# Encoder layer with expert retrieval on one core: ranking products from 16-bit halves, another order inside the dense chunks, three GpSimd transfers issued later

## The chip, the cores and the metric

One Trainium2 chip, of which the kernel uses one core. The metric is device time in microseconds of one execution; lower is better. Engines are named as in the profile: PE is TensorE (PEld its weight loads), DVE VectorE, ACT ScalarE, POOL GpSimd, SP SyncE, which only issues transfers.

## What is computed

One encoder layer on 512 tokens of 1024 values in float32: attention first (not touched by the change), then retrieval of experts, cut here to what matters:

```python
def peer(h, w_query, sub_keys, expert_u, expert_v):      # h: 512 x 1024 after norm
    q = (h @ w_query).reshape(512, 8, 2, 128)             # 8 heads, 2 halves
    s = einsum('chpd,hpnd->chpn', q, sub_keys)            # 128 keys for each half
    top_s, top_i = top_k(s, 16)                           # 16 best of each half
    cand_s = top_s[..., 0, :, None] + top_s[..., 1, None, :]
    cand_i = top_i[..., 0, :, None] * 128 + top_i[..., 1, None, :]
    best_s, pos = top_k(cand_s.reshape(512, 8, 256), 16)  # 16 experts per token and head
    idx = take_along_axis(cand_i, pos)
    g = softmax(best_s)
    act = gelu(einsum('cd,chkd->chk', h, expert_u[idx]))
    return einsum('chk,chkd->cd', g * act, expert_v[idx])
```

A residual add and a last RMSNorm follow.

## The kernel before

**Routing, eight heads one after the other (`route`).** For each head the keys are ranked by how strongly the tokens ask for them: `rank0` multiplies the 128 keys of each half with the 512 queries (`pst`, one 128x512 float32 product, line 1206), ACT sums the exponentials of the result, and DVE (`rank1`, `rank2`) turns these sums into ranks. The ranks only decide which expert goes which way: 512 pairs of high-ranked keys (the cells of `RECTS`, four chunks of 128 experts) are computed for all tokens, which is the dense part; every other pair that a token chose is fetched for that token alone, which is the tail. `scores`, computed in full float32 (`sps`), are what the result is made of.

**Dense chunks (`dense`).** 8 heads of 4 chunks make 32 chunks. For a chunk, a gather on POOL (`load_u`) brings 128 expert rows `du`. They are worked on one chunk ahead, in halves `hh` of 512 values: `turn` transposes a half on PE into the PSUM tile `ut` (line 1531) and ACT casts it to the upper part `uh` (line 1534); `low` lets PE subtract `uh` in place from `ut` (line 1541) and ACT casts what is left to `ul` (line 1542). The 24 products of the chunk before (`udot`, line 1549) are cut into four quarters of 6, and ahead of each quarter stands one of the four steps, in the order turn 0, low 0, turn 1, low 1. `gelu` on ACT and `weigh` on DVE make weights `gT` of the products, and when a head's four chunks are through, `outputs` multiplies them with the four gathered value tiles `dv` (`vacc`, 64 records of line 1600) and DVE adds the result to `accd`. `values` issues the gathers for `dv`; the four `dv` buffers are used again by each head, so a gather for the next head waits until the `vacc` products have read the old rows.

**Tail (`tail`).** While the dense part of heads 0 to 7 goes on, 75 tail columns are worked through beside it. The tokens are sorted by how many tail pairs they have and form four blocks; a fifth small block, "fold", takes the pairs that exceed the blocks' columns. Each column is two gathers on POOL, `tid` (the expert's number) and `tuv` (its rows, 8 KB per token, 6 buffers), a dot product on DVE (`tscr`, line 1900), two short steps on ACT (`twg`, lines 1820 and 1821) and one more pass on DVE (`tacc`, line 1822). A block's results are scattered to `zs` (line 2027) after DVE has added them (`tx`); `ENDS` names the columns of the next block at which its end is advanced.

**What sets the order.** From the routing on, every engine's instructions keep the order in which the program emits them (`in_order`). In the tail phase `interleave` emits tail loads and columns between the quarters of the dense part, by estimated costs. So ACT has the casts of the dense chunks and the `twg` steps of the tail in one queue, and POOL has the gathers of both.

Of the kernel before, what the change touches and what calls it, by code (L numbers as in the profile page):

```python
# [52 lines left out]
JOINS = 1  # L53
JPOOL = (2,)
LEAD = 0.0
ENDS = (2, 4, 5)
LASTDN = (3.4,)
BIG = 4096.0

# [1110 lines left out]
class Head:  # L1170
# [29 lines left out]
    def rank0(self, p):  # L1200

        nc, R = self.nc, self.R
        if p == 0:
            self.stat = R.tile([128, 2], F32, name="stat", bufs=2)
        ps = self.G.PS.tile([128, T], F32, name="pst", tag="rank")
        nc.tensor.matmul(ps, self.keys[:, 0, p], self.q[p], start=True, stop=True)
        junk = R.tile([128, T], BF16, name="pexp", bufs=1)
        nc.scalar.activation(junk, ps, AF.Exp, scale=KEYSCALE, accum_out=self.stat[:, p:p + 1])

# [296 lines left out]
def dense(tc, A, G, DN):  # L1506

    nc = tc.nc
    G.ready = []
    G.nident = DN.tile([128, 128], F32R, name="nident")  # L1510
    nc.scalar.activation(G.nident, G.ident, AF.Copy, scale=-1.0)
    uv = A["UV"].rearrange("e (k d) -> (e k) d", k=2)
    n = NHEAD * NCH
    us, parts, ws, acts = {}, {}, {}, {}

    def weights(h):
        assert h in G.stored
        for j in range(NCH):
            ws[h, j] = DN.tile([128, T], F32, name="gT", bufs=NCH)
            nc.sync.dma_start(ws[h, j], G.gts[h, j])  # L1520

    def load_u(c):
        us[c] = DN.tile([128, D], F32, name="du", bufs=4)
        gather(nc, us[c], uv, G.cids[c // NCH][:, 0, c % NCH:c % NCH + 1])

    def turn(c, hh):

        u = us[c]
        pt = G.PD[hh % len(G.PD)].tile([128, 4, 128], F32, name="ut")
        for k in range(4):  # L1530
            nc.tensor.matmul(pt[:, k], u[:, (hh * 4 + k) * 128:(hh * 4 + k + 1) * 128], G.ident,  # L1531
                             is_transpose=True, start=k == 0, stop=False, skip_group_check=True)
        uh = DN.tile([128, 4, 128], F32R, name="uh", bufs=4)
        nc.scalar.copy(uh, pt)  # L1534
        parts[c, hh] = pt, uh

    def low(c, hh):

        pt, uh = parts[c, hh]
        ul = DN.tile([128, 4, 128], F32R, name="ul", bufs=4)  # L1540
        nc.tensor.matmul(pt, G.nident, uh, start=False, stop=True, skip_group_check=True)  # L1541
        nc.scalar.copy(ul, pt)  # L1542
        parts[c, hh] = ul, uh

    def dots(c, ps, k0, k1):
        for k in range(k0, k1):
            ul, uh = (t[:, k % 4] for t in parts[c, k // 4])
            for i, (a, b) in enumerate(((uh, G.hH), (uh, G.hL), (ul, G.hH))):
                nc.tensor.matmul(ps, a, b[:, k], start=k == 0 and i == 0, stop=k == KC - 1 and i == 2)  # L1549

    def gelu():
        for c, ps in G.pending:
            acts[c] = DN.tile([128, T], F32, name="act", bufs=2)
            nc.scalar.activation(acts[c], ps, AF.Gelu)
        G.pending.clear()

    G.gelu, G.pending = gelu, []

    def weigh(c):
        if c in acts:  # L1560
            w = ws[divmod(c, NCH)]
            nc.vector.tensor_tensor(w, acts.pop(c), w, op=OP.mult)

    def values(c):
        h, j = divmod(c, NCH)
        vs[j] = DN.tile([128, D], F32, name="dv", bufs=NCH)
        gather(nc, vs[j], uv, G.cids[h][:, 1, j:j + 1])

    def add(h, b, hh, ps):
        dst = G.accd[:, b, hh * 512:(hh + 1) * 512]  # L1570
        if h == 0:
            nc.vector.tensor_copy(dst, ps)
        elif h < NHEAD - 1:
            nc.vector.tensor_tensor(dst, dst, ps, op=OP.add)  # L1574
        else:
            tmp = DN.tile([128, 512], F32, name="vgf", tag="act", bufs=2)
            nc.vector.tensor_tensor(tmp, ps, G.gf[:, hh * 512:(hh + 1) * 512], op=OP.mult)
            nc.vector.tensor_tensor(dst, dst, tmp, op=OP.add)
            if hh == 1:
                G.ready.append(b)  # L1580

    def flush_adds():
        while G.adds:
            add(*G.adds.pop(0))

    G.adds, G.hold, G.flush_adds = [], False, flush_adds

    def outputs(h):

        for b in range(NB):  # L1590
            for hh in range(2):
                if len(G.adds) == sum(G.vbufs):
                    add(*G.adds.pop(0))
                if hh == 0 and (h + 1) * NCH + b + 2 < n:
                    load_u((h + 1) * NCH + b + 2)
                i = 0 if len(G.PD) == 1 or (b * 2 + hh) % 3 else 1
                ps = G.PD[i].tile([128, 512], F32, name="vacc", bufs=G.vbufs[i])
                sl = slice(hh * 512, (hh + 1) * 512)
                for k in range(NCH):
                    nc.tensor.matmul(ps, ws[h, k][:, b * 128:(b + 1) * 128], vs[k][:, sl], start=k == 0, stop=k == NCH - 1)  # L1600
                while G.adds and not G.hold:
                    add(*G.adds.pop(0))
                G.adds.append((h, b, hh, ps))
                yield PE_OUT, (DM_ROWS if hh == 0 else 0.0), VE_STEP * (2 if h == NHEAD - 1 else 1)
        flush_adds()
        if h + 1 < NHEAD:
            weights(h + 1)
            values((h + 1) * NCH)

    for c in range(4):  # L1610
        load_u(c)
    yield 0.0, 0.0, 0.0
    for hh in range(2):
        turn(0, hh)
        yield PE_CHUNK / 4, 0.0, 0.0
        low(0, hh)
        yield PE_CHUNK / 4, 0.0, 0.0
    load_u(4)
    vs = {}
    for c in range(n):  # L1620
        h, j = divmod(c, NCH)
        gelu()
        if len(G.PD) == 1 and c % 2:
            ps = G.PD[0].tile([128, T], F32, name="udot2", tag="vacc", bufs=2)
        else:
            ps = G.PD[j % len(G.PD)].tile([128, T], F32, name="udot")
        for k in range(4):
            if c + 1 < n:
                (low if k % 2 else turn)(c + 1, k // 2)
            if c == 0 and k == 3:  # L1630
                load_u(5)
            dots(c, ps, 2 * k, 2 * k + 2)
            if k == 2:
                weigh(c - 1)
            if k == 3 and c == 0:
                weights(0)
            if k < 3:
                yield PE_CHUNK / 4, 0.0, VE_STEP if k == 2 else 0.0
        G.pending.append((c, ps))
        if not G.defer:  # L1640
            gelu()
        if c == 0 or j > 0:
            values(c)
        if h == NHEAD - 1 and j > 0:
            for b in range(NB) if j == 1 else ():
                nc.vector.tensor_tensor(G.accd[:, b], G.accd[:, b], G.gf, op=OP.mult)
        if c == n - 1:
            gelu()
            weigh(c)
        yield PE_CHUNK / 4, DM_ROWS + DM_W, 0.0  # L1650

        if j == 0 and h > 0:
            yield from outputs(h - 1)
    yield from outputs(NHEAD - 1)


# [248 lines left out]
def tail(tc, A, G, TL, out):  # L1905
# [7 lines left out]
    def prepare(i):  # L1913

        if i == "fold":
            yield from fold_rows(tc, G, TL)
        cd, hp = tail_rows(tc, G, TL, G.permx if i == "fold" else G.perm[:, i:i + 1])
        if i == TORDER[0]:
            blocks[i] = tail_block(tc, TL, cd, hp, None, TAIL[i], G.first)
            return  # L1920
        yield
        yield
        cw = TL.tile([128, NL], F32, name="tcw", bufs=1)
        code = TL.tile([128, 40], F32, name="tcode", bufs=3)
        if i == "fold":
            xs = TL.tile([128, MOST], F32, name="txs", bufs=1)
            yield from tail_codes(nc, xs, cd[:, 0:NL], cw, MOST)
            for k in range(FOLD):
                junk = TL.tile([128, MOST], F32, name="txj", bufs=1)
                nc.vector.scalar_tensor_tensor(junk, iom, G.foff[:, k:k + 1], xs, op0=OP.is_equal, op1=OP.mult,  # L1930
                                               accum_out=code[:, k:k + 1])
        else:
            yield from tail_codes(nc, code, cd[:, 0:NL], cw, TAIL[i])
        blocks[i] = tail_block(tc, TL, cd, hp, code, FOLD if i == "fold" else TAIL[i])
# [29 lines left out]
    def load():  # L1964

        n = t.nuv
        if t.nb < len(starts):
            left = starts[t.nb] - (n + IDLEAD)
            for _ in range((2 if left < 11 else 0) if left > 1 else 99):
                if next(coming[t.nb], 0) == 0:  # L1970
                    t.nb += 1
                    break
# [151 lines left out]
```

## Time and profile before

| what | us |
|---|---|
| three timed runs | 1061.93, 1062.4, 1075.23 |
| their median | 1062.4 |
| the profiled execution, its own time | 1061.16 |
| span of the profiled execution, first to last instruction | 1059.4 |
| PE busy in it | 954.7 (90%) |
| DVE busy | 774.6 (73%) |
| POOL busy | 523.3 (49%) |
| ACT busy | 430.9 (41%) |

The span is 1.8 us shorter than the execution's own time. Attention takes the first 335 us, routing with the first dense chunks reaches to about 597 us, the tail phase to about 1033 us, and the last norm closes. Idle time of an engine costs something only where the end waits for it.

### The profile page before, as it was taken

To read this page: it belongs to the slowest core of one execution; us is meant where nothing else is said; L and a number is where in the kernel's file an instruction comes from. 1 tells how busy PE (TensorE), PEld (TensorE's weight loads), DVE (VectorE), ACT (ScalarE), POOL (GpSimd) and SP (SyncE) were. 2 spreads that over 40 slices of the span, in tenths; PEclk is the share of its full clock that TensorE was granted. 3 is DMA by queue.
4 is the path that set the end of the run, shared out by engine and by line. 5 is a ranking of instruction groups with operands and counts; after the bars stand their busy time and mean duration, and the time that the engine had idled before them with its cause. 6 is when DMAs were issued, how large, how long until landed. Compare 5 with 4: busy or idle time off the path is not lost.

```text
span 1059.4 us, 13188 instructions
## 1 busy us (share of the span) xinstructions
PE 954.7 (90%) x4038; PEld 625.7 (59%) x4038; DVE 774.6 (73%) x2238; ACT 430.9 (41%) x941; POOL 523.3 (49%) x572
## 2 busy tenths in 40 slices
PE   7899989998999999999977879999998997999992
PEld 2476548776898545666653455564655655475651
DVE  4538656888637369989998667987577765677887
ACT  3333366556415346667775322241412322232212
POOL 1145611324322146666667437685567737277513
PEclk9999989999999999999988879999999998999997
DMA  8554132422211643654324568875869948578652
GB/s 335 187 226 156 63 139 71 170 88 72 80 41 60 224 140 101 160 140 120 91 71 109 172 243 300 318 253 197 307 240 391 336 161 302 175 282 280 217 185 81
DMA packets 76372, 192.91 MB, mean 182 GB/s; under 512 B 23205, under 2 KB 40997, under 8 KB 64805
## 3 DMA queue, kind: packets, MB, share of 16 engines
q0 software_dynamic: 25344, 112.90, 29.9%
q1 hardware_dynamic: 50232, 78.50, 22.7%
q10 hardware_dynamic: 720, 0.62, 0.2%
q8 instruction: 32, 0.52, 0.2%
q14 instruction: 44, 0.36, 0.1%
HBM read 181.66 MB, written 18.96 MB: 189 GB/s over the span
## 4 chain that ended last, share of the span: by engine, by line
PE 59%; DVE 18%; issue 5%; DMA 2%; ACT 2%; POOL 1%; another core or an unknown queue 0%; DVEq 0%; POOLq 0%; ACTq 0%
PE vacc L1600 18%; PE udot L1549 14%; PE q L1193 7%; PE outp L308 4%; PE ops L834 3%; PE ut L1531 2%; PE sc L810 2%; PE pt L818 2%; PE ut L1541 1%; DVE dexp L1419 1%; DVE tscr L1900 1%; DVE tacc L1822 1%; DMA wraw_pq<-in_w_pq 1%; PE gtp L1426 1%; PE sc L806 1%
## 5 line engine op out<-in xcount | busy, mean ns | idle before, releaser
L1600 PE MATMUL vacc<-dv,gT 128*128 128x512 f32 x512 | 228.4, 605 | 3.1 <-DVE accd L1574 2.3
L1600 PEld LDWEIGHTS vacc<-dv,gT 128*128 128x128 f32 x512 | 98.9, 194 | 124.8 <-issue 116.6
L1822 DVE SCALAR_TENSOR_TENSOR tacc<-tuv,twg,tacc 128x1024 f32<-128x1024 f32 x75 | 96.3, 1284 | 38.9 <-ACT twg L1821 30.5
L1900 DVE SCALAR_TENSOR_TENSOR tscr<-tuv,thp 128x1024 bf16<-128x1024 f32 x75 | 91.4, 1219 | 29.0 <-DMA tuv<-in_UV,tid 27.0
L1549 PE MATMUL udot<-hH,uh 128*128 128x512 f32 x256 | 110.8, 433 | 0.0
L1549 PE MATMUL udot<-hH,ul 128*128 128x512 f32 x256 | 105.1, 410 | 0.0
L1549 PE MATMUL udot<-hL,uh 128*128 128x512 f32 x256 | 104.8, 409 | 0.0
L159 POOL DMA_INDIRECT tuv<-in_UV,tid x75 | 92.2, 1229 | 23.6 <-issue 16.7
L159 POOL DMA_INDIRECT tid<-tab,tci x75 | 89.8, 1197 | 28.5 <-issue 22.9
L1193 PE MATMUL q<-hx,wraw_pq 128*128 128x512 f32 x208 | 94.0, 593 | 0.0
L1534 ACT CAST uh<-ut 128x512 fp32r<-128x512 f32 x64 | 37.3, 583 | 90.3 <-PE ut L1531 41.1
L330 POOL TENSOR_TENSOR ada_acc<-ada_acc,ada_w 128x1024 f32<-128x1024 f32 x9 | 21.4, 2383 | 83.9 <-ACT ada_w L329 28.7
L1820 ACT ACTIVATE twg<-tdots 128x1 f32<-128x1 f32 x75 | 15.1, 202 | 117.1 <-DVE tscr L1900 90.1
L1193 PEld LDWEIGHTS q<-hx,wraw_pq 128*128 128x128 f32 x208 | 38.1, 190 | 39.7 <-issue 39.2
L159 POOL DMA_INDIRECT dv<-in_UV,cid x32 | 36.8, 1151 | 49.4 <-PE vacc L1600 41.1
L812 ACT ACTIVATE psb<-psb,anm 128x512 f32<-128x512 f32 (+2 forms) x64 | 40.9, 640 | 48.1 <-DVE psb L811 32.3
L300 POOL TENSOR_TENSOR wl_in<-wraw_in,wh_in 128x1024 fp32r<-128x1024 f32 x10 | 25.6, 2558 | 70.6 <-ACT wh_in L299 70.6
L1549 PEld LDWEIGHTS udot<-hH,ul 128*128 128x128 f32 x256 | 50.4, 197 | 12.7 <-issue 0.2
L1549 PEld LDWEIGHTS udot<-hH,uh 128*128 128x128 f32 x256 | 50.9, 199 | 9.5 <-issue 1.4
L1549 PEld LDWEIGHTS udot<-hL,uh 128*128 128x128 f32 x256 | 50.6, 198 | 9.6 <-issue 0.2
L1542 ACT CAST ul<-ut 128x512 fp32r<-128x512 f32 x64 | 37.4, 585 | 45.8 <-PE ut L1541 37.1
L1541 PE MATMUL ut<-uh,nident 128*128 128x512 f32 x64 | 30.6, 479 | 25.1 <-issue 22.3
(401 smaller groups left out, 2243.6 us busy)
## 6 DMA issues: line engine op xcount, KB each, us to landing
ada_w<-in_w_ada SPq DMA_DIRECT2D x22, 1024.0 KB
wraw_pq<-in_w_pq SPq DMA_DIRECT2D x16, 512.0 KB
gts<-gts SPq DMA_DIRECT2D x32, 256.0 KB
gT<-gts SPq DMA_DIRECT2D x32, 256.0 KB
wraw_in<-in_w_in SPq DMA_DIRECT2D x10, 512.0 KB
wraw_out<-in_w_out SPq DMA_DIRECT2D x8, 512.0 KB
x1T<-in_xT SPq DMA_DIRECT2D x4, 512.0 KB
ada_w<-in_w_ada SPq DMA_DIRECT2D x4, 512.0 KB
```

What stands on the lines that cost most here:

```text
L159: nc.gpsimd.indirect_dma_start(out=out, out_offset=None, in_=src, in_offset=bass.IndirectOffsetOnAxis(ap=idx, axis=0), **kw)
L308: nc.tensor.matmul(ps, a[:, c], b[:, c], start=n == 0, stop=n == 3 * kc - 1)
L812: nc.scalar.activation(U.p, U.p, AF.Exp, bias=nm, scale=-1.0, accum_out=B.den[:, i:i + 1])
L834: nc.tensor.matmul(B.ops[U.grp][:, U.h], U.pt[:, j], vr, start=j == 0, stop=j == U.nk - 1)
L1193: nc.tensor.matmul(self.q[p][:, cols], w[:, c], x[:, c, cols], start=c == 0, stop=c == KC - 1)
L1534: nc.scalar.copy(uh, pt)
L1541: nc.tensor.matmul(pt, G.nident, uh, start=False, stop=True, skip_group_check=True)
L1542: nc.scalar.copy(ul, pt)
L1549: nc.tensor.matmul(ps, a, b[:, k], start=k == 0 and i == 0, stop=k == KC - 1 and i == 2)
L1600: nc.tensor.matmul(ps, ws[h, k][:, b * 128:(b + 1) * 128], vs[k][:, sl], start=k == 0, stop=k == NCH - 1)
L1822: nc.vector.scalar_tensor_tensor(acc, uv[:, D:], wg, acc, op0=OP.mult, op1=OP.add)
L1900: nc.vector.scalar_tensor_tensor(B.s, uv[:, 0:D], 1.0, B.hp, op0=OP.mult, op1=OP.mult, accum_out=B.dots[:, c])
```

## The change

Six edits. (1) `rank0` multiplies only the upper 16 bits of each float32 word, seen as bfloat16 with a step of two, so that one 16-bit product takes the place of a float32 product; there are 16 of them. Ranks are made from these shortened products; the scores stay as they are. (2) In the tail phase the four steps ahead of the quarters of a chunk stand in the order turn 0, turn 1, low 0, low 1 (the two halves have a PSUM tile each there). (3) The first `dv` gather of a head is no longer emitted at the end of `outputs` but ahead of the third quarter of the next chunk. (4) The block for the folded pairs waits two steps more before its two gathers, and (5) the steps that prepare a block start one load earlier. (6) The scatter of a block's result is emitted at column 8 of the next block, not 5.

```diff
@@ -53,7 +53,7 @@
-ENDS = (2, 4, 5)
+ENDS = (2, 4, 8)
@@ -1203,7 +1203,7 @@
         ps = self.G.PS.tile([128, T], F32, name="pst", tag="rank")
-        nc.tensor.matmul(ps, self.keys[:, 0, p], self.q[p], start=True, stop=True)
+        nc.tensor.matmul(ps, self.keys[:, 0, p].bitcast(BF16)[:, 1::2], self.q[p].bitcast(BF16)[:, 1::2], start=True, stop=True)
         junk = R.tile([128, T], BF16, name="pexp", bufs=1)
@@ -1605,7 +1605,7 @@
         flush_adds()
         if h + 1 < NHEAD:
             weights(h + 1)
-            values((h + 1) * NCH)
+            G.soon = (h + 1) * NCH
@@ -1624,9 +1625,15 @@
+        ahead = ((turn, 0), (turn, 1), (low, 0), (low, 1)) if len(G.PD) > 1 and (c + 1, 0) not in parts else \
+            ((turn, 0), (low, 0), (turn, 1), (low, 1))
         for k in range(4):
             if c + 1 < n:
-                (low if k % 2 else turn)(c + 1, k // 2)
+                ahead[k][0](c + 1, ahead[k][1])
+            if k == 2 and G.soon is not None:
+                values(G.soon)
+                G.soon = None
@@ -1914,6 +1921,8 @@
         if i == "fold":
             yield from fold_rows(tc, G, TL)
+            yield
+            yield
@@ -1966,7 +1975,7 @@
-            for _ in range((2 if left < 11 else 0) if left > 1 else 99):
+            for _ in range((2 if left < 12 else 0) if left > 1 else 99):
```

**ACT inside two chunks of the tail phase.** The names carry buffer numbers here: before, `ut_6377` and `ut_6410` are the first and the second half of one chunk. Before:

```order
L1534 CAST uh_6382<-ut_6377 128x512
L1820 ACTIVATE twg_5688<-tdots_5687 128x1
L1821 ACTIVATE twg_5688<-twg_5688,tgate_5686 128x1
L1542 CAST ul_6401<-ut_6377 128x512
L1534 CAST uh_6415<-ut_6410 128x512
L1542 CAST ul_6424<-ut_6410 128x512
L1554 ACTIVATE act_6433<-udot_6376 128x512
```

The same stretch of ACT's queue now, with `ut_6401` as the second half:

```order
L1534 CAST uh_6382<-ut_6377 128x512
L1827 ACTIVATE twg_5688<-tdots_5687 128x1
L1828 ACTIVATE twg_5688<-twg_5688,tgate_5686 128x1
L1534 CAST uh_6406<-ut_6401 128x512
L1542 CAST ul_6414<-ut_6377 128x512
L1542 CAST ul_6424<-ut_6401 128x512
L1554 ACTIVATE act_6433<-udot_6376 128x512
```

The cast of the second half's upper part moved ahead of the first half's lower part; both lower parts now stand behind the tail column's `twg`.

**POOL at the `vacc` products of head 4, as a difference.** `cid5` are the expert numbers of the next head:

```order
+L159 DMA tcd_7440<-cdg_2778,perm_2785 128x800
+L159 DMA thp_7442<-hs_2776,perm_2785 128x1024
 L159 DMA tid_6295<-tab_2774,tci_6294 128x1
 L159 DMA tuv5_5678<-in_UV,tid_6295 128x2048
-L159 DMA dv_7460<-in_UV,cid5_4561 128x1024
-L159 DMA tcd_7485<-cdg_2778,perm_2785 128x800
-L159 DMA thp_7487<-hs_2776,perm_2785 128x1024
 L159 DMA tid_6295<-tab_2774,tci_6294 128x1
 L159 DMA tuv0_5673<-in_UV,tid_6295 128x2048
-L159 DMA dv_7525<-in_UV,cid5_4561 128x1024
+L159 DMA dv_7512<-in_UV,cid5_4561 128x1024
+L159 DMA dv_7532<-in_UV,cid5_4561 128x1024
```

The first `dv` gather now stands behind the two gathers of a new tail block and one more tail column (`tid`, `tuv`). At the other heads it moved past one or two tail columns.

**POOL at the scatter of a block's result.** Before:

```order
L159 DMA tuv0_5673<-in_UV,tid_6295 128x2048
L2027 DMA zs_2777<-tx1_6787,perm_2785 512x1024
L159 DMA du_6923<-in_UV,cid4_4219 128x1024
L159 DMA tid_6295<-tab_2774,tci_6294 128x1
L159 DMA tuv1_5674<-in_UV,tid_6295 128x2048
```

The same scatter now:

```order
L159 DMA tid_6295<-tab_2774,tci_6294 128x1
L159 DMA tuv3_5676<-in_UV,tid_6295 128x2048
L2036 DMA zs_2777<-tx1_6787,perm_2785 512x1024
L159 DMA du_6987<-in_UV,cid5_4561 128x1024
L159 DMA tid_6295<-tab_2774,tci_6294 128x1
```

The scatter moved behind the loads of three more columns (`tuv1` to `tuv3`) and two `du` gathers. The fold block's two gathers stand on POOL where they stood, behind the load of `tuv4`; the DVE and PE steps that they wait for are emitted one column earlier.

## Rows read from the trace of the kernel before

**Rows 1.** The page: PE's granted clock by fortieths of the span, in tenths.
```profile
PEclk9999989999999999999988879999999998999997
```

**Rows 2.** Busy time by stretches: start:end, length, engines, clock, DMA share, GB/s.
```profile
core 0: us, PE busy (x) PEld busy (x) DVE busy (x) ACT busy (x) POOL busy (x), PEclk, DMA share, GB/s
395.00:425.00 30.00, 27.87 (x107) 15.55 (x106) 28.96 (x161) 21.44 (x45) 20.32 (x44) 1.00 0.39 113
465.10:492.13 27.03, 27.03 (x113) 17.15 (x113) 24.68 (x136) 20.60 (x39) 16.59 (x33) 1.00 0.49 140
...
604.00:632.00 28.00, 19.50 (x67) 15.12 (x67) 15.77 (x51) 6.97 (x16) 12.74 (x15) 0.70 0.75 298
800.00:836.00 36.00, 30.47 (x138) 23.64 (x137) 24.89 (x45) 13.44 (x32) 28.16 (x26) 0.95 0.99 385
...
863.00:906.00 43.00, 34.85 (x142) 26.40 (x141) 25.19 (x49) 14.42 (x34) 34.17 (x30) 0.88 0.86 307
933.00:961.00 28.00, 28.00 (x137) 22.64 (x136) 20.59 (x36) 13.22 (x31) 22.30 (x19) 1.00 0.86 304
```

**Rows 3.** PE's waits, 597 to 1060 us: total, times, longest.
```profile
PE ut L1541 <- issue: 22.3, 8, 7.0
PE ut L1541 <- ACT uh L1534: 2.6, 2, 1.3
```

**Rows 4.** PE's timeline, longest waits ahead of line 1541: start, duration, operation, [idle before].
```profile
605.30 0.50 PE L1541 MATMUL ut<-uh,nident 128*128 128x512 f32 x1 [2.28 <-issue]
...
621.55 0.80 PE L1541 MATMUL ut<-uh,nident 128*128 128x512 f32 x1 [7.05 <-issue]
...
811.60 0.79 PE L1541 MATMUL ut<-uh,nident 128*128 128x512 f32 x1 [2.59 <-issue]
...
818.85 0.50 PE L1541 MATMUL ut<-uh,nident 128*128 128x512 f32 x1 [1.99 <-issue]
...
884.93 0.79 PE L1541 MATMUL ut<-uh,nident 128*128 128x512 f32 x1 [4.19 <-issue]
885.52 0.63 PE L1549 MATMUL udot<-hH,uh 128*128 128x512 f32 x1
885.95 0.63 PE L1549 MATMUL udot<-hL,uh 128*128 128x512 f32 x1
```

**Rows 5.** ACT's timeline ahead of the 4.19 us wait.
```profile
882.11 0.60 ACT L1554 ACTIVATE act<-udot 128x512 f32<-128x512 f32 x1 [3.66 <-PE udot L1549]
884.29 0.58 ACT L1534 CAST uh<-ut 128x512 fp32r<-128x512 f32 x1 [1.58 <-issue]
```

**Rows 6.** The chain that ended last, 465 to 493 us: start, length, what.
```profile
471.96 0.86 PE pst L1206 x2
472.82 0.23 PE ut L1541
473.05 1.40 PE udot L1549 x6
...
478.74 0.44 PE ut L1531 x4
```

**Rows 7.** DVE's timeline in the same head: its waits.
```profile
477.08 0.43 DVE L1214 TENSOR_SCALAR pbits<-stat 128x2 int32<-128x2 int32 x1 [1.30 <-ACT pexp L1208]
...
480.84 0.35 DVE L1229 TENSOR_SCALAR_CACHE_REDUCE pjunk<-psc,pkey 128x128 bf16<-128x128 f32 x1 [0.40 <-PE psc L1224]
```

**Rows 8.** POOL's longest waits, 600 to 1060 us.
```profile
POOL zs L2027 <- DVE tx L2025: 44.3, 4, 19.7
POOL dv L159 <- PE vacc L1600: 41.1, 6, 15.5
...
POOL tcd L159 <- DVE nmax L1790: 16.3, 1, 16.3
```

**Rows 9.** ACT's longest waits, 600 to 1060 us.
```profile
ACT twg L1820 <- DVE tscr L1900: 90.1, 22, 8.5
```

**Rows 10.** The same waits inside one `vacc` stretch, 836 to 863 us.
```profile
ACT twg L1820 <- DVE tscr L1900: 16.1, 4, 6.3
```

More of the change, by code (lines that the diff above doesn't have):

```diff
@@ L1626, in dense @@
             ps = G.PD[j % len(G.PD)].tile([128, T], F32, name="udot")
+        ahead = ((turn, 0), (turn, 1), (low, 0), (low, 1)) if len(G.PD) > 1 and (c + 1, 0) not in parts else \
+            ((turn, 0), (low, 0), (turn, 1), (low, 1))
         for k in range(4):
             if c + 1 < n:
-                (low if k % 2 else turn)(c + 1, k // 2)
+                ahead[k][0](c + 1, ahead[k][1])
+            if k == 2 and G.soon is not None:
+                values(G.soon)
+                G.soon = None
             if c == 0 and k == 3:
```

## The prediction, made before the changed kernel ran

> **What bounds the kernel now.** I read the page first: PE is the busiest engine by far, and its clock sags in a few places [rows 1]. So I asked for the busy time by stretches, to see where PE is not the limit [rows 2], then for what PE waits for in the tail phase [rows 3], and where [rows 4]. The reader is to see three regimes.
>
> In the routing heads PE is full, 27.03 of 27.03 us, at the upper clock level, but DVE has only 2.35 us of the 27.03 left, and in an earlier head it is itself the limit with 28.96 of 30 [rows 2]. PE and DVE are nearly equal bounds there.
>
> In an undisturbed stretch of the tail phase, 933 to 961 us, four chunks run with PE full for 28 us. The same work took 36 us at 800 and 43 us at 863 [rows 2], and these differences are what can be won. Nearly all of it sits ahead of one line: PE waits ten times for the cast `uh` before it can run `low`, 24.9 us in all [rows 3], with a longest wait of 7.05 us [rows 4].
>
> After a long wait the clock falls as well: behind the 4.19 us wait one product follows the last after 0.43 us (885.52 to 885.95) [rows 4], while six products take 1.40 us in the chain, 0.23 each [rows 6]. [...]
>
> Why the cast is late the trace does not settle. Ahead of the 4.19 us wait ACT runs nothing for 3.66 us, then `act`, and again nothing for 1.58 us before `uh` [rows 5], although the transposes stand six products ahead of PE's wait, which by then had lasted 3.5 us [rows 4]. In these two stretches DMA and POOL are nearly full: 0.99 and 0.86 of the DMA engines, and POOL's 26 and 30 instructions take 28.16 of 36 and 34.17 of 43 us [rows 2].
>
> **Edit 1, the shortened ranking products.** A float32 product costs PE 0.86 us in the chain, a one-pass product of the same 512 columns (`low`) 0.23 [rows 6]. No 512-column bfloat16 product is in the trace, and none that reads every second 16-bit word. Its price lies between 0.23 and 0.86; I take 0.23, because `low` is the row with the same columns in one pass. The gain is 0.63 for each of 16 products, at most 10.1 us. The explicit weight load could add up to 0.19 us each, 3 us in all, if nothing covered it; I take zero, since the loads of the float32 products ran under other products.
>
> [...]
>
> How much of the 10.1 reaches the end is decided by DVE. In a steady head DVE waits 1.30 us for the exponentials behind the products and 0.40 us for the transposes behind them [rows 7]. Both shrink when the two products shrink by 1.26 us together, so the three steady heads give 1.26 each, 3.8. In the two heads around 395 to 425 us DVE is the limit [rows 2], and I count nothing. Heads 0, 1 and 7 have one or two of the products in the open: 0.6, 1.3 and 0.6. Sum 6.3 us, bounds -3 and 10.1.
>
> **Edit 2, the order of the four steps.** Before, six products (1.40 us) stand between a `turn` and its `low`, and the cast takes 0.58 of them [rows 5, 6]. PE waits as soon as ACT is more than 0.8 us late. Now a further step and six more products lie between: 0.44 + 1.40 = 1.84 us more for the first half [rows 6]; the second half gains 0.23 + 1.40 = 1.63, and I use 1.84 for all. Each wait then shrinks by 1.84 or vanishes. Five waits are longer than that, 2.28, 7.05, 2.59, 1.99 and 4.19 [rows 4], and leave 0.44 + 5.21 + 0.75 + 0.15 + 2.35 = 8.9 us. Of 24.9 us [rows 3], 16.0 go. What the order takes elsewhere is slack: `low` of the first half now ends one quarter ahead of the products that read `ul`, not two. That leaves 1.40 + 0.23 + 1.40 - 0.58 = 2.45 us for ACT, still three times the old smallest margin, and I cost it at nothing unless ACT is held longer than that (first rival).
>
> With the waits some of the low clock goes. Its price: at 800, PE is busy for 30.47 us with work that takes 28.0 undisturbed, 2.5; at 863, 34.85 less 28.0 and less about 2 for the four fold products there, 4.9; at 604 the mean clock of 0.70 over 28 us means 16.8 us at the lower level, of which some 7 are the wait itself, so 9.8 / 2 = 4.9 [rows 2]. Together 12.3 us. The two longest waits stay partly, so I take half, 6; bounds 0 and 12.3.
>
> **Edits 3 to 6, the transfers.** POOL takes its queue in order, and behind a waiting gather stand the loads of the next tail columns. It waits 41.1 us in six places for the `vacc` products, 44.3 us at the four scatters, 16.3 us once at the fold block [rows 8]. Moving these later lets POOL run one to three columns further before it stops. That helps only if a `tuv` buffer is free, and with six buffers POOL has usually filled them when it stops. At head 4 the move is largest: two gathers of a block and a column go ahead of a 15.5 us wait, and the crowded stretch at 863 follows. Bounds: -3 us (the scatter of a block comes later and nothing is gained) and +6; I take 1. The `dv` rows are needed only by the next `vacc` products, a whole set of chunks later, so their delay costs nothing.
>
> **What is late next.** In the two bad stretches POOL is full if its 0.3 us gaps between instructions count: 28.2 + 7.8 = 36 of 36 us and 34.2 + 9 = 43 of 43 [rows 2]. If PE needs only 28 and 30 us there, the tail columns cannot all come as early, and since DVE and ACT take columns and dense work from one queue, PE will wait for some of them. One to three POOL instructions of 1.3 us move out of each; some 4 us stay in each stretch. I take 6 us back, bounds 0 and 16.
>
> **Sum.** 6.3 + 16.0 + 6 + 1 - 6 = 23.3 us off. Against the profiled execution's 1061.16 that is 1037.9; it ran 1.2 us under the median of the runs shown, so I say 1039 us.
>
> **Rivals.** First, *the slack is not what was missing*: whatever holds ACT holds it longer than the new margin, or shifts with PE, and since both `ul` casts now stand behind `twg`, a held ACT stops PE at the products instead of at `low`. For it: ACT was late twice in a row ahead of the 4.19 us wait [rows 5], which a margin of one quarter does not cover, and ACT waits 90.1 us in 22 places for DVE's dot product [rows 9]. Against it: these waits lie in the `vacc` stretches, where no cast is due (16.1 us in one of them alone [rows 10]), and ahead of the 4.19 us wait no `twg` stands at all [rows 5]. Only edit 1 and a little would remain, 8 us: 1054. [...]
>
> Second, *everything goes*: all 24.9 us of waits, the 12.3 us of clock and the steady part of edit 1, 6.3; 43.5 off, 1019. For it: the undisturbed stretch at 933 runs with 0.86 of the DMA engines busy and no wait [rows 2]. Against it: POOL's full stretches.
>
> Third, *slower*: the late `ul` casts stop PE at each late column. With 22 waits of 4.1 us on average [rows 9] less the margin of 2.45, that is 36 us of PE waits instead of 24.9, with clock loss in proportion, 18 instead of 12.3, and edit 1 not reaching the end: 17 slower than now, and with a second wait in one of the crowded stretches 22 or more, 1084. It decides from the point at which most of the 22 waits fall into chunks; against it, they now lie beside the `vacc` products [rows 10].
>
> **How the numbers follow.** Chances: forecast 0.57, slack not missing 0.25, everything goes 0.13, slower 0.05. Low end: edit 1 at 10.1, 24.9 of waits gone and nothing late next gives 1022 with part of the clock. High end: edit 1 alone at 6, the rest nothing, 1056. That range holds most of the forecast and of the first rival and a little of the second, 8 in 10. A change of 2%, 21 us, is about what a measurement of this kernel can tell from no change; faster than 1041 are two thirds of the forecast and all of the second rival: 0.52. Slower 0.05, within 0.43.
>
> **What would show it.** Edit 1 is right if a `pst` product takes about 0.23 us in the chain and DVE's waits in a routing head fall below 0.5 us; if the head still takes 27 us, DVE was the bound. Edit 2 is right if the waits ahead of line 1541 fall under 10 us and the clock at 800 and 863 stays at the upper level; the first rival is right if as many microseconds of wait stand ahead of the `udot` products. The transfers are right if POOL's waits at `dv` and `zs` fall and the stretch at 863 has no `tuv` that DVE waits for. The forecast fails if the lateness of ACT comes from something that shifts with PE, so that each cast is late by the same amount after a `turn` however much room there is.

## The result, and the profile after

The changed kernel ran 1034.67 us (median of four, 1032.97 to 1040.31), the kernel before beside it 1068.82 us (1061.93 to 1075.48). The ratio is 0.969 with an interval of 0.960 to 0.978: faster by 3.1%, near the 1039 us forecast. The profiled execution took 1034.5 us, its span is 1032.6 us, and its mean granted clock 0.966 against 0.957.

This comparison has to be read with one made later. On three other occasions, on chips numbered 14, 2 and 7, the unchanged kernel took not 1062 but 1034.7 to 1037.8 us (medians of 25 to 35 executions), and on chip 2 the changed kernel took 1022.71 us: ratio 0.985, interval 0.980 to 0.991. Both intervals lie below 1, so the change is faster on both occasions, but by half as much on the second.

First the changed kernel of the first comparison. The page's clock row, beside [rows 1]: the dip of [rows 1] at 874 to 900 us is gone, those between some 520 and 645 us are still there.

```profile
PEclk9999999999999999999988988999999999999997
```

Busy time by stretches, columns as in [rows 2]: a steady routing head, the first chunks of the tail phase, then the stretches that answer to 800, 836 and 863 us.

```profile
core 0: us, PE busy (x) PEld busy (x) DVE busy (x) ACT busy (x) POOL busy (x), PEclk, DMA share, GB/s
493.12:518.91 25.79, 25.79 (x111) 16.50 (x110) 24.55 (x133) 19.65 (x37) 16.57 (x33) 1.00 0.34 93
597.00:626.00 29.00, 18.20 (x70) 13.63 (x69) 18.78 (x62) 8.31 (x16) 15.32 (x18) 0.74 0.80 308
787.00:823.00 36.00, 36.00 (x157) 26.34 (x156) 29.65 (x55) 13.77 (x34) 24.34 (x20) 1.00 0.84 300
823.00:850.00 27.00, 27.00 (x64) 11.92 (x63) 20.86 (x36) 3.33 (x13) 19.84 (x17) 1.00 0.89 318
850.00:881.00 31.00, 30.32 (x142) 23.59 (x141) 25.19 (x50) 14.49 (x34) 25.21 (x20) 1.00 0.83 283
```

A head takes 25.79 us where it took 27.03. From 787 to 881 us PE is nearly full at a granted clock of 1.00; in [rows 2] it was busy for 30.47 of 36 and 34.85 of 43 us. POOL works 19.84 of 27 us beside the `vacc` products, where it worked 9.66 in the kernel before:

```profile
836.00:863.00 27.00, 27.00 (x64) 11.92 (x63) 20.89 (x36) 3.25 (x13) 9.66 (x8) 1.00 0.48 167
```

But the first chunks of the tail are no better: 18.20 us of work in 29, clock 0.74. What PE waits for in the tail phase (total, times, longest), beside [rows 3]:

```profile
PE ut L1531 <- issue: 11.9, 2, 8.8
...
PE ut L1541 <- issue: 0.9, 1, 0.9
PE ut L1541 <- ACT uh L1534: 0.9, 2, 0.6
```

The 24.9 us ahead of `low` have become 1.8, and 11.9 us have appeared where the old kernel had none, ahead of `turn` of the following chunk: it overwrites the PSUM tile that the late cast `ul` still has to read. The timeline there, PE, then ACT, then DVE:

```profile
616.39 1.12 PE L1531 MATMUL ut<-ident,du 128*128 128x128 f32 x4 [8.78 <-issue]
...
608.52 0.29 ACT L1828 ACTIVATE twg<-twg,tgate 128x1 f32<-128x1 f32 x1
615.76 0.59 ACT L1542 CAST ul<-ut 128x512 fp32r<-128x512 f32 x1 [6.95 <-remote]
...
615.72 0.16 DVE L1764 COPY fscr<-foldp 128x4 f32<-128x4 f32 x1 [6.32 <-remote]
```

ACT and DVE stand for 6.95 and 6.32 us and go on within 0.04 us of each other; "remote" means that the trace finds no releaser on this core. POOL's and ACT's waits, beside [rows 8, 9]:

```profile
POOL dv L159 <- PE vacc L1600: 41.1, 6, 10.8
...
POOL zs L2036 <- DVE tx L2034: 15.1, 1, 15.1
...
POOL tcd L159 <- DVE nmax L1797: 9.9, 1, 9.9
...
ACT twg L1827 <- DVE tscr L1907: 85.0, 21, 8.8
```

The scatter's waits fell from 44.3 us in four places to 15.1 in one; the sum at `dv` is unchanged.

**Where the time came from**, by the starts of the `vacc` products of each head in the profiled executions, in us. "Routing" runs from the first `pst` to head 0's `vacc`, "tail start" from there to head 2's, the other columns from one head's `vacc` to the next.

| kernel | routing | tail start | 2 to 3 | 3 to 4 | 4 to 5 | 5 to 6 | 6 to 7 |
|---|---|---|---|---|---|---|---|
| before, first comparison | 201.7 | 159.6 | 63.0 | 63.1 | 70.1 | 55.2 | 51.1 |
| after, first comparison | 196.8 | 162.5 | 63.0 | 55.2 | 57.9 | 55.2 | 49.6 |
| e5, before | 202.5 | 155.7 | 63.0 | 55.8 | 57.9 | 55.2 | 51.1 |
| e6, after | 196.5 | 147.9 | 63.0 | 55.2 | 57.9 | 55.2 | 49.6 |
| e1, edit 1 | 198.7 | 154.2 | 63.0 | 56.3 | 57.9 | 55.2 | 51.1 |
| e2, edit 2 | 202.4 | 154.1 | 63.1 | 56.2 | 57.9 | 55.2 | 49.6 |
| e3, edits 3 to 6 | 201.7 | 146.1 | 63.0 | 55.2 | 57.9 | 55.2 | 51.1 |
| e4, edits 2 to 6 | 201.9 | 146.0 | 63.0 | 55.2 | 57.9 | 55.2 | 49.6 |
| e7, edit 6 | 201.7 | 152.9 | 63.0 | 55.3 | 57.9 | 55.2 | 51.1 |
| e8, edit 3 | 202.5 | 154.3 | 63.0 | 55.3 | 57.9 | 55.2 | 51.1 |
| e9, edits 4 and 5 | 202.7 | 148.2 | 67.1 | 55.3 | 57.9 | 55.2 | 51.1 |
| e10, edit 5 | 202.1 | 150.4 | 63.0 | 55.3 | 57.9 | 55.6 | 51.1 |
| e11, edit 4 | 202.0 | 154.8 | 63.0 | 55.6 | 57.9 | 55.2 | 51.1 |
| e12, edits 1, 2, 3, 6 | 198.9 | 150.2 | 63.0 | 55.2 | 57.9 | 55.2 | 49.6 |

In the first comparison the span fell by 26.8 us: 4.9 in routing, 3.0 before it (the first `pst` came at 345.30 us, not at 348.34; over all runs it comes anywhere from 345.2 to 351.7, with the same code ahead of it), 2.9 lost at the tail start, 7.9 and 12.2 won at heads 3 to 5, 1.5 in the last stretch. The 20 us at heads 3 to 5 are most of it, and in every run of a later occasion, the unchanged kernel's included, these stretches are already short. Between e5 and e6 the span falls by 13.3 us: 6.0 in routing, 7.8 at the tail start, 0.6 and 1.5 in two later stretches, and some 2.7 are lost outside the table.

### The profile page after: what moved, and what is told of

The parts are those of the page before. It is cut to its first block, busy times and chain, and to the rows that moved or that the text cites. A ratio compares the mean times of both kernels' runs of the same rounds, so it can differ in the third digit from the quotient of the medians.

```text
span 1032.6 us, 13163 instructions
## 1 busy us (share of the span) xinstructions
PE 933.3 (90%) x4022; PEld 614.3 (59%) x4022; DVE 777.9 (75%) x2238; ACT 430.2 (42%) x941; POOL 534.6 (52%) x572
## 4 chain that ended last, share of the span: by engine, by line
PE 58%; DVE 17%; issue 3%; DMA 3%; POOL 2%; ACT 2%; another core or an unknown queue 1%; SPq 0%; DVEq 0%; POOLq 0%; ACTq 0%
PE vacc L1600 18%; PE udot L1549 15%; PE q L1193 6%; PE outp L308 4%; PE ops L834 3%; PE ut L1531 2%; PE sc L810 2%; PE pt L818 1%; DVE dexp L1419 1%; PE ut L1541 1%; DMA wraw_pq<-in_w_pq 1%; DVE psb L811 1%; DVE ti L1295 1%; DMA tuv<-in_UV,tid 1%; DVE ti L1291 1%
## 5 line engine op out<-in xcount | busy, mean ns | idle before, releaser
L159 POOL DMA_INDIRECT tuv<-in_UV,tid x75 | 94.6, 1261 | 28.2 <-issue 14.9
L159 POOL DMA_INDIRECT dv<-in_UV,cid x32 | 39.2, 1224 | 48.6 <-PE vacc L1600 41.1
L1827 ACT ACTIVATE twg<-tdots 128x1 f32<-128x1 f32 x75 | 15.2, 202 | 111.2 <-DVE tscr L1907 85.0
L1531 PE MATMUL ut<-ident,du 128*128 128x128 f32 x256 | 40.1, 281 | 16.1 <-issue 11.9
```

Source lines behind the costliest of these rows:

```text
L159: nc.gpsimd.indirect_dma_start(out=out, out_offset=None, in_=src, in_offset=bass.IndirectOffsetOnAxis(ap=idx, axis=0), **kw)
```

## The experiments

All were timed beside the kernel before on the same chip. The ratio is to that kernel, and microseconds are worked out from the ratio. Where the interval holds 1 (e1, e2, e5, e7, e8, e10, e11), the measurement doesn't tell the run from the kernel before. The times expected for e1 to e4 were set against 1062 us, while the kernel before ran at 1035.59; so these four are judged by what they say of the difference.

**e1 to e4 (chip 14; before 1035.59 us).** Which edits carry the gain? e1 is the kernel before with the changed product in `rank0` alone:

```diff
-        nc.tensor.matmul(ps, self.keys[:, 0, p], self.q[p], start=True, stop=True)
+        nc.tensor.matmul(ps, self.keys[:, 0, p].bitcast(BF16)[:, 1::2], self.q[p].bitcast(BF16)[:, 1::2], start=True, stop=True)
```

> The kernel before with edit 1 alone. Theory (terms add, edit 1 worth about 6 us): 1.000 to 0.990 of the kernel before, about 1055 against 1061; the milestones of routing (start of the last head's q products) 4 to 7 us earlier, and the tail phase as before, with the waits ahead of line 1541 still above 20 us. Rival A (edit 1 matters more, since it shifts the tail phase against the transfers): the tail phase itself becomes shorter, waits ahead of line 1541 under 10 us, and the time is 1045 or less. Rival B (DVE was the bound in routing): no gain, 1061.

Measured: 1034.06 us, ratio 0.998 (0.993 to 1.003). The interval holds the theory's 6 us as well as nothing. In the profiles, routing is 3.8 us shorter than e5's, and the tail start moved by no more than it does between other runs. The waits at line 1541 are 7.0 us, but rival A's reading of that falls with e5, where the unchanged kernel has 8.6.

e2 has the new order of the four steps alone:

```diff
-                (low if k % 2 else turn)(c + 1, k // 2)
+                ahead[k][0](c + 1, ahead[k][1])
```

> The kernel before with edit 2 alone. Theory (the missing slack was the main cost): waits ahead of line 1541 under 5 us, clock at the upper level from 800 to 906 us, 16 to 20 us faster than before, about 1043. Rival (the moved transfers removed the crowding, the order by itself only shifts the wait): waits ahead of line 1531 or of the udot products take over with 10 us or more, and the time is within 8 us of before, 1053 or more.

Measured: 1034.59 us, ratio 0.998 (0.994 to 1.001). The theory's 16 to 20 us are not there; by time the rival is right, but its mechanism only partly: one wait of 4.7 us ahead of line 1531 is what came in place of the 8.6 us that e5 has ahead of line 1541.

```profile
PE ut L1531 <- ACT ul L1542: 4.7, 1, 4.7
```

The one lasting difference is 1.5 us in the stretch from head 6 to 7, which every kernel with this edit shows and none without.

e3 has edits 3 to 6 alone:

```diff
-ENDS = (2, 4, 5)
+ENDS = (2, 4, 8)
-            values((h + 1) * NCH)
+            G.soon = (h + 1) * NCH
+            if k == 2 and G.soon is not None:
+                values(G.soon)
+            yield
+            yield
-            for _ in range((2 if left < 11 else 0) if left > 1 else 99):
+            for _ in range((2 if left < 12 else 0) if left > 1 else 99):
```

> The kernel before with edits 3 to 6 alone (dv gathers, fold block, preparing of a block, scatter). Theory: POOL's waits at dv and zs fall as in the changed kernel, the waits ahead of line 1541 stay above 15 us, and the time is within 4 us of before, 1057 to 1063. Rival (the transfers were the cause): the stretch of head 5, which is 12 us shorter in the changed kernel, is shorter here too, and the time is 1048 or less.

Measured, in only four executions: 1026.55 us, ratio 0.990 (0.983 to 0.997), some 11 us. The theory (within 4 us of before) falls by the median, though the interval begins at 3.6 us. The rival's place was wrong too: in the profile the gain lies at the tail start (146.1 us), not at head 5.

e4 is the changed kernel with the old float32 product.

> The changed kernel without edit 1, that is the kernel before with edits 2 to 6. Theory (terms add): 4 to 6 us slower than the changed kernel, about 1040. Rival (order and transfers work only at the phase that the shorter routing gives): 1050 or more, with waits ahead of line 1541 or 1531 above 10 us.

Measured: 1027.67 us, ratio 0.992 (0.988 to 0.996). That is 7 us less than the whole change wins in e6, a little above the 4 to 6 expected; but e6 ran on another chip, and the intervals (4.1 to 12.4 us here, 9.3 to 20.9 there) overlap. Beside e3, the new order adds nothing that this measurement can tell.

**e5 and e6 (chip 2; before 1037.84 us).** Both kernels unchanged, to repeat the comparison with profiles.

> The kernel before, unchanged, for a profile beside the others. The runs of the last call had it at 1035.6 us (25 executions), not at 1062. Theory C (what cost 27 us in the first profile were disturbances of those executions, waits of ACT whose releaser the trace does not show, and not the kernel's order): about 1035, waits ahead of line 1541 of 7 to 10 us with ACT named as releaser, and the stretches of heads 4 and 5 about 56 and 58 us from one vacc stretch to the next, as in the run with edit 1 alone. Rival D (edit 1 had changed these stretches): about 1035 but with heads 4 and 5 still above 60 us.

> The changed kernel beside the kernel before on one chip. Theory C (the true effect is that of the transfers, about 9 us, plus 2 for each of the first two edits, partly overlapping): 1022 to 1027, ratio 0.987 to 0.992. Rival E (the ratio of 0.969 of the first comparison is the kernel's): 1003 to 1008.

Measured: e5 1035.2 us, ratio to itself 0.998 (0.995 to 1.002); e6 1022.71 us, ratio 0.985 (0.980 to 0.991). Theory C holds for e5; for e6 its time holds, and the ratio lies a little below its 0.987. D and E fall. In e5 the trace names the releaser of every wait ahead of line 1541, so it shows why casts are late on this occasion. The unchanged kernel, e5: PE, ACT, DVE and POOL at the start of the tail.

```profile
618.72 0.80 PE L1541 MATMUL ut<-uh,nident 128*128 128x512 f32 x1 [5.39 <-ACT uh L1534]
...
616.69 0.20 ACT L1820 ACTIVATE twg<-tdots 128x1 f32<-128x1 f32 x1 [7.62 <-DVE tscr L1900]
...
618.08 0.59 ACT L1534 CAST uh<-ut 128x512 fp32r<-128x512 f32 x1
...
615.42 1.23 DVE L1900 SCALAR_TENSOR_TENSOR tscr<-tuv,thp 128x1024 bf16<-128x1024 f32 x1 [6.76 <-DMA tuv<-in_UV,tid]
...
618.99 0.74 DVE L1749 TENSOR_TENSOR fscr<-fscr 128x1 f32<-128x1 f32 x4
...
633.23 0.96 POOL L159 DMA_INDIRECT tcd<-cdg,permx  x1 [13.16 <-DVE nmax L1790]
```

Follow the chain from its cause: the first tail column's rows land late, DVE's dot product `tscr` waits 6.76 us for them, ACT's `twg` waits 7.62 us for that product, the casts of the dense chunk stand behind `twg` in ACT's queue, and PE waits 5.39 us. ACT ran nothing in the 7.62 us up to 616.69, though PE had come to `low` and stood for `uh` from 613.33 on (618.72 less 5.39); `uh` ran at 618.08, behind `twg`. Behind the same `tscr` stand DVE's steps for the fold block (`fscr`, at their end `nmax`), with three more columns between them, and POOL waits 13.16 us at `tcd` for `nmax` and issues no tail load meanwhile. The changed kernel, e6, the same place:

```profile
610.43 0.66 PE L1531 MATMUL ut<-ident,du 128*128 128x128 f32 x4 [1.59 <-ACT ul L1542]
...
609.37 0.20 ACT L1827 ACTIVATE twg<-tdots 128x1 f32<-128x1 f32 x1 [6.71 <-DVE tscr L1907]
...
603.81 0.74 DVE L1756 TENSOR_TENSOR fscr<-fscr 128x1 f32<-128x1 f32 x4
...
608.11 1.23 DVE L1907 SCALAR_TENSOR_TENSOR tscr<-tuv,thp 128x1024 bf16<-128x1024 f32 x1 [2.48 <-DMA tuv<-in_UV,tid]
...
620.33 0.96 POOL L159 DMA_INDIRECT tcd<-cdg,permx  x1 [4.02 <-DVE nmax L1797]
```

ACT is held nearly as long (6.71 us), but PE loses 1.59 instead of 5.39. Edit 2's slack is one part of that, not all: with edit 2 alone (e2) 4.7 us remain, and with the transfers alone (e3) the waits ahead of line 1541 are 4.3 us in four places. The first steps of the fold block (`fscr`) now run ahead of the first `tscr`, where they ran behind it, and POOL's wait falls to 4.02 us: that is edits 4 and 5, which e9 to e11 take apart. Of PE's waits in the tail phase, the longest line for `ut` in e5:

```profile
PE ut L1541 <- ACT uh L1534: 8.6, 4, 5.4
```

and in e6:

```profile
PE ut L1531 <- ACT ul L1542: 1.6, 1, 1.6
```

Two stretches of e5 that answer to 800 and 863 us of [rows 2]; PE is full or nearly so, and the clock is at 1.00, in the unchanged kernel:

```profile
796.00:824.00 28.00, 28.00 (x138) 22.75 (x137) 23.83 (x44) 13.31 (x32) 22.21 (x20) 1.00 0.99 383
...
854.00:882.00 28.00, 27.32 (x128) 21.20 (x127) 22.14 (x43) 13.36 (x33) 21.91 (x21) 1.00 0.81 286
```

**e7 and e8 (same chip and runs of before).** Which of the transfers? e7 has edit 6 alone (`ENDS`), e8 edit 3 alone (`G.soon`).

> The kernel before with edit 6 alone (the scatter at column 8 of the next block). Theory F (the 9 us of the transfers come from the scatter, which held POOL 33.8 us in four places and in the run with edits 3 to 6 only 15.6 us in one): 6 us or more faster than before, ratio 0.994 or lower, POOL's waits at zs below 20 us, and the first tail stretch (from the start of head 0's vacc to head 1's) shorter by 4 us or more. Rival G (they come from the dv gathers, edit 3): within 2 us of before, ratio above 0.997.

> The kernel before with edit 3 alone (the first dv gather of a head emitted ahead of the third quarter of the next chunk). Theory F: within 2 us of before, ratio above 0.997. Rival G: 6 us or more faster, ratio 0.994 or lower, the waits of POOL at dv unchanged in sum at some 35 us but with two or three more tail columns issued ahead of each, and the second tail stretch shorter by 4 us or more. If neither reaches 0.994, the fold block (edits 4 and 5) is the cause or the parts work only together.

Measured: e7 1037.1 us, ratio 1.000 (0.998 to 1.003); e8 1032.93 us, ratio 0.998 (0.995 to 1.001). F and G both fall as causes by themselves. POOL's waits fit that. In e5:

```profile
POOL zs L2027 <- DVE tx L2025: 32.4, 4, 12.6
POOL dv L159 <- PE vacc L1600: 32.1, 6, 11.2
```

In e7:

```profile
POOL dv L159 <- PE vacc L1600: 47.6, 7, 10.7
...
POOL zs L2027 <- DVE tx L2025: 12.7, 1, 12.7
```

In e8:

```profile
POOL zs L2031 <- DVE tx L2029: 44.0, 4, 14.0
...
POOL dv L159 <- PE vacc L1600: 20.2, 5, 9.9
```

In e5 that is 64.5 us together. Moving the scatter takes the one to 12.7 and brings the other to 47.6, 60.3 together; moving the gather does the opposite, 64.2. It looks as if a POOL that doesn't stop at the one runs on and stops at the other. With both moved the sum is 54.8 in e3 and 49.6 in e12.

**e9 to e12 (chip 7; before 1034.7 us).** The fold block: e9 has edits 4 and 5, e10 edit 5 (`left < 12`), e11 edit 4 (the two `yield` steps), and e12 is the changed kernel without both.

> The kernel before with edits 4 and 5 alone (the fold block's two gathers two steps later, the preparing steps one load earlier). Theory H (the gain of edits 3 to 6 comes from here: the DVE steps of the fold block no longer stand behind the first tail dot product, which waits some 7 us for its rows, so POOL, which stood 13.2 us at tcd in the profile of the kernel before, goes on loading): 6 us or more faster than before, ratio 0.994 or lower, POOL's wait at tcd below 5 us, and the start of head 1's vacc products (704.98 us in the kernel before) at 698 us or earlier. Rival I (the three moves work only together): ratio above 0.997.

> Edit 5 alone (the preparing steps one load earlier, the two gathers then also one load earlier in POOL's queue). Theory H says that it is the earlier DVE steps that count: ratio 0.994 or lower, as with both edits, POOL's wait at tcd about one load (2.6 us) longer than with both, so 5 to 8 us. Rival K (what counts is that the gathers stand further back on POOL): no gain, ratio above 0.997.

> Edit 4 alone (the two gathers one load later on POOL, the DVE steps where they were). Theory H: POOL's wait at tcd shorter by about one load, 13 to 10 us, and the time within 3 us of before, ratio above 0.997. Rival K: 6 us or more faster, ratio 0.994 or lower.

> The changed kernel without edits 4 and 5. Theory H: the gain shrinks from about 15 to about 6 us, ratio 0.992 to 0.998, with POOL standing 10 us or more at tcd again. Rival I (everything works only together, or edits 1 and 2 carry the gain): either no gain at all, above 0.998, or still below 0.988.

| run | median us | ratio | interval | POOL at `tcd`, us |
|---|---|---|---|---|
| e9 | 1033.07 | 0.997 | 0.995 to 1.000 | 4.0 |
| e10 | 1032.74 | 0.999 | 0.996 to 1.001 | 8.8 |
| e11 | 1036.53 | 1.000 | 0.998 to 1.002 | 7.2 |
| e12 | 1028.21 | 0.994 | 0.991 to 0.997 | 8.5 |

Theory H was right about the waits with both edits and wrong in its size: neither e9 nor e10 reaches the ratio of 0.994, and by time alone e9 (0.9973) falls to rival I. In e9 POOL's wait is 4.0 us and head 2's `vacc` (the expectation calls it head 1's) begins 7.5 us earlier after head 0's than in e5 (148.2 against 155.7), as expected, but the runs are only 2.8 us faster (0.3 to 5.2). In the profiled execution 4.1 us of that went again between heads 2 and 3, 67.1 us instead of 63.0. The products with which the fold block is joined, in e9:

```profile
728.39 1.13 PE L1950 MATMUL foldp<-tacc,fold 128*128 128x512 f32 x2 [1.03 <-DVE tacc L1822]
730.30 1.86 PE L1950 MATMUL foldp<-tacc,fold 128*128 128x512 f32 x2 [0.78 <-DVE tacc L1954]
732.94 2.08 PE L1950 MATMUL foldp<-tacc,fold 128*128 128x512 f32 x2 [0.78 <-DVE tacc L1954]
735.69 2.08 PE L1950 MATMUL foldp<-tacc,fold 128*128 128x512 f32 x2 [0.68 <-ACT tacc L1952]
```

and in e3, with the same four waits:

```profile
725.21 1.13 PE L1954 MATMUL foldp<-tacc,fold 128*128 128x512 f32 x2 [1.03 <-DVE tacc L1826]
727.12 1.13 PE L1954 MATMUL foldp<-tacc,fold 128*128 128x512 f32 x2 [0.78 <-DVE tacc L1958]
729.02 1.12 PE L1954 MATMUL foldp<-tacc,fold 128*128 128x512 f32 x2 [0.78 <-DVE tacc L1958]
730.83 1.12 PE L1954 MATMUL foldp<-tacc,fold 128*128 128x512 f32 x2 [0.68 <-ACT tacc L1956]
```

The pairs of products take 1.86 and 2.08 us in e9 and 1.13 in e3. Twelve microseconds from just before the first pair show the clock (the third number from the end), in e9:

```profile
728.00:740.00 12.00, 9.38 (x16) 3.98 (x17) 5.16 (x10) 1.76 (x3) 9.62 (x8) 0.61 0.96 357
```

and in e3:

```profile
725.00:737.00 12.00, 9.55 (x35) 5.68 (x36) 5.07 (x11) 3.72 (x8) 9.56 (x9) 1.00 0.96 360
```

So in e9 the granted clock was 0.61 on average there, against 1.00 in e3. One profile doesn't tell how often that happens. In e10, with edit 5 alone, POOL's wait of 8.8 us is no less than the 8.5 to 13.2 of the later runs with neither edit, and the time shows no gain: that it is the earlier DVE steps that count, as H had it, is not shown. e11 says that moving the gathers back is worth nothing that can be told alone (1.000, 0.998 to 1.002), though the wait is shorter than expected (7.2 us): rival K falls. e12 wins 6.4 us (3.6 to 9.2) where the changed kernel won 15.2 on another chip, which is what H expected, with POOL's wait at 8.5 us a little under its 10. So e12 speaks for H and against I, and e9 the other way round: that edits 4 and 5 matter beside the others is shown by e12, how much they are worth is not settled.

**The sum of the parts.** Edits 1, 2, 3, 6 and 4 with 5, each alone, make -2.2, -2.5, -2.2, +0.4 and -2.8 us, 9.3 together; the whole change makes 15.2 (9.3 to 20.9). The transfers (edits 3, 6, and 4 with 5) make 4.6 apart and 10.9 (3.6 to 18.0) together in e3. It looks as if they do more together than apart, but the intervals allow plain addition. The tail-start column speaks against a surplus: set against e5, one profile, edits 6, 3 and 4 with 5 alone are 2.8, 1.4 and 7.5 us shorter, 11.7 in sum, and e3 is 9.6.

## Why the prediction was right, and where it was not

**Edit 1: right in price.** A ranking product takes 0.23 us in the chain after, where it took 0.86:

```profile
467.49 0.23 PE pst L1206
467.71 0.23 PE ut L1541
```

Two steady heads of the first comparison shrank by 1.24 us each (27.03 to 25.79), forecast 1.26; in e1 and e6 three take 25.87 to 26.35, from one head's first `pst` to the next's. Over the whole of routing the gain is 4.9 us in the first comparison, 6.0 between e5 and e6 and 3.8 between e5 and e1, forecast 6.3. That much of it reaches the end is not shown: edit 1 alone made 2.2 us (-3.1 to 7.4). Of DVE's waits at `pbits`, 1.3 us remain in one steady head and 0.6 in the next, so "below 0.5" was too low. The step of four bytes shows no cost in the trace: this product takes 0.23 us like `low`. Its weight load takes 0.10 us (16 loads), where one of the float32 product took 0.19 in the trace before (32 loads, 5.7 us together).

**Edit 2: the mechanism is seen, its size is not.** In the first comparison the waits ahead of line 1541 fell from 24.9 to 1.8 us, under the 10 that were named as the sign. As many microseconds ahead of `udot` did not come, but 11.9 came ahead of `turn`, which neither the forecast nor the first rival had named: net 11.2 us of the 16.0. The first rival's cause, casts held behind `twg`, is what e5 shows at the start of the tail; its result (1054) did not come. Whether edit 2 removed the 24.9 us is not shown either: on the later occasions the unchanged kernel has only 8.6 us of these waits. There the edit alone left 4.7 us of waits and made 2.5 us (-1.0 to 6.0), where 16.0 for the waits and 6 for the clock were forecast.

**The clock: as expected, but no proof.** At 800 and 863 us it is back at 1.00, as the sign had it; but it is so in the unchanged kernel of e5 as well, so this sign doesn't tell the change from the occasion. The forecast took the lower clock as half of the upper; in the trace before it is 0.50 from 885.40 to 890.00 us. At the tail start it is still 0.74, behind the new 8.78 us wait.

**The transfers: the step that failed most clearly.** I took 1 us, with 3 lost and 6 won as bounds; e3 measured 10.9 (3.6 to 18.0). I had priced POOL's waits by how far POOL would run ahead, and had looked at head 4. In the profiles the gain lies at the tail start, where POOL stopped at `tcd` (16.3 us [rows 8]) and issued no tail load. That row stood in the prediction's own list, but edits 4 and 5 were priced as moving two gathers, not as moving the DVE steps that they wait for ahead of a dot product that waits for DMA. This stop is one part of the gain: without edits 4 and 5 the tail start of e12 is 5.5 us shorter than e5's as well.

**What is late next: wrong.** I gave 6 us back because POOL looked full in the two bad stretches. Nothing became late there: heads 3 to 4 and 4 to 5 take 55.2 and 57.9 us in the changed kernel, and 55.2 to 56.3 and 57.9 in all runs of the later occasions. What was given back, 2.9 us, fell at the tail start.

**Why 1039 was near: partly luck.** The forecast was 23.3 us off; the first comparison measured 33 (23 to 43), the second 15.2 (9.3 to 20.9). It was made against an execution that had 20 us in heads 3 to 5 to lose, and the changed kernel lost none there on the same occasion. That these 20 us are the kernel's is not shown: on three other occasions the unchanged kernel ran at 1034.7 to 1037.8, and its trace (e5) doesn't have them. There edit 1, edit 2 and the transfers make 2.2, 2.5 and 10.9 us, where 6.3, 22 and 1 were forecast with 6 given back: terms missed in both directions. What differed on the first occasion are the "remote" waits. ACT's waits at the two casts in the kernel before:

```profile
ACT uh L1534 <- remote: 9.9, 3, 4.4
...
ACT ul L1542 <- remote: 2.0, 1, 2.0
```

and in the changed kernel:

```profile
ACT ul L1542 <- remote: 11.0, 2, 6.9
```

These are 11.9 and 11.0 us, and the traces of e1 to e12 show none in the tail phase. The changed kernel of the first comparison is also 11 us behind e6. The 12 us that the kernel before loses from head 4 to 5 come behind POOL's 15.5 us wait at `dv` [rows 8]; the reading that one late stretch there led to the next is argued from the order of the rows and was not tested. What holds ACT in the "remote" waits, whether the chip or the hour brought them, and which edit, if any, kept heads 3 to 5 whole on that occasion, stays open: no later run met them.

## What to carry to other kernels

When the queue of one engine mixes work of two kinds, follow a late step back through the queues to the transfer that it really waits for; here the same late rows held ACT's casts, DVE's preparing steps and POOL's next loads, and emitting short steps ahead of the waiting one, with the waiting gathers moved back, cut a stop of POOL from 13.16 to 4.02 us that no busy share pointed to. Moving one stop of a queue may only send it to the next stop, as in e7 and e8, where 64.5 us of POOL's waits became 60.3 and 64.2; count its waits together, not one by one. A stretch that is bad in one profiled execution is to be seen in a second one, on another chip if possible, before a sum is built on it.

## What the runs showed of the hardware

- In e4 the time went with the granted clock: of its ten executions, five with a mean clock of 0.971 to 0.974 took 1023.7 to 1024.8 us, the other five at 0.958 to 0.965 took 1030.6 to 1035.7.
- Through the same four waits of 0.68 to 1.03 us between short pairs of products the clock stayed at 1.00 in one kernel (e3) and fell to a mean of 0.61 in another (e9); that stretch was 4.1 us longer.
- Waits for which the trace has no releaser on the core, 6.32 us on DVE and 6.95 us on ACT, ended within 0.04 us of each other in a program that uses one core.
